# A hybrid decoder block: two orders pinned in the seven-product blocks, and a row factor with two sets of columns

## The chip, the cores and the metric

The kernel runs on one core of one Trainium2 chip. The metric is the device time of one execution in microseconds (us). The core's engines are TensorE (PE in the profile; PEld is its weight load), VectorE (DVE), ScalarE (ACT), GpSimd (POOL) and SyncE (SP), which here issues the loads of the weights.

## The reference

One layer over x of 256 tokens by 2048 channels, all in fp32: a half-step FFN, a mixer, a second half-step FFN, a final norm.

```python
def swiglu_ffn(x, w_gate, w_up, w_down):
    return (jax.nn.silu(x @ w_gate) * (x @ w_up)) @ w_down

x = x + 0.5 * swiglu_ffn(rms_norm(x, ffn1_norm), ffn1_w_gate, ffn1_w_up, ffn1_w_down)
z = rms_norm(x, mix_norm) @ w_in          # recurrent branch and short convolution follow
...
x = x + y @ w_out
x = x + 0.5 * swiglu_ffn(rms_norm(x, ffn2_norm), ffn2_w_gate, ffn2_w_up, ffn2_w_down)
return rms_norm(x, final_norm)
```

The gate and up weights are 2048 x 5632, the down weights 5632 x 2048.

## The kernel before

**The precision.** Every operand of a product is held as a high part (a cast to fp32r) and a low part (the rest). `parts_of` (line 170) makes both from a weight tile `raw` of 128 x 2048 elements, which is a block of 512 rows by 512 columns: ScalarE casts it in two halves (`hi`), then VectorE subtracts (`lo`). `multiply` (line 197) multiplies a weight block with 128 tokens in 12 matmuls: eight with the high part, for which the stationary operand is in turn the tokens' high and low part, then four with the low part. So TensorE meets the high part first and the low part 8 matmuls later.

**The seven products.** Gate and up weights are taken in 11 columns of 512 (`s` counts pairs of columns behind the first, 0 to 4), and in four row units of 512 (`u`). `seven` (line 345) does for a pair of columns and row units 0 and 1, with both halves of the tokens, what would be eight block products, by seven, with sums of weight blocks and prepared sums of the tokens (`sf`, tiles `xs`). Units 2 and 3 of the same columns go by `usual`, plain products for both token halves. The weight blocks are w11, w12 (unit 0, first and second column), w21, w22 (unit 1), and for the usual ones b2, a2 (unit 2), b3, a3 (unit 3). The program's order of one block is:

- p0: w11 into bank a (copied to d)
- w11 := w12 - w11 on VectorE, then p4 with it into bank c: the **second product**
- x01: b2 into banks e and c
- w11 := w22 - w11, then p5 into a
- x11: b3 into e and c
- w12 := w22 - w12, the **fourth's weight sum**, then p6 into a: the fourth product
- p2: w22 into c
- x00: a2 into d and a
- w11 := w21 - w11, then p3 into a; x10: a3 into a and d; p1: w21 into d

That is 180 matmuls. A block is named after its matrix, FFN and pair: g1_2 is the gate of FFN1, s = 2; u2_0 the up of FFN2, s = 0; d1_5 and the like are blocks of the down product. There are 20 of g and u and 6 of d. The tiles carry it: lo_g1_2_p4 is the low part of the second product of g1_2, raw_u1_1_01 the w12 of u1_1 (row unit, then column: 00 is w11, 01 w12, 11 w22, 10 w21, 21 and 31 are b2 and b3, 20 and 30 a2 and a3). In the profile the numbers of blocks are left out (lo_g_p, raw_u). Gate and up of a pair alternate: g1_0, u1_0, g1_1, u1_1 and on, with a block of the down product behind every second pair.

**Buffers and loads.** A load is 1 MB from the SP queue (line 165), in the order that the scheduler set; a load at the head of the queue waits until its buffer is free, and those behind it wait too. w11 and w12 lie in a pool of 2 (tag `kept`): the next block's w11 goes where this block's w12 lies and is free after lo p6; the next w12 goes where w11 lies and is free after lo p3. The others share a pool of 3 (tag `raw`). High and low parts have three buffers in turn.

**The order of work.** The program is written through wrappers whose call sits on line 43, so nearly all instructions of the profile carry L43, and tiles tell them apart. A scheduler sets the order of each engine by its own model of durations, with the dependences as bounds. `tc.keep_in_program_order(ins)` adds a bound: ins stays behind the instruction that the program wrote last before it for the same engine. Before the change this was used in `join` (line 440) and, for all instructions, at the start of FFN1 and at the end of the last down product.

**The row factor.** The mixer and FFN2 normalise after the product has begun. `Norm.rows` (line 254) spreads the factor of each token over the partitions: per token half it multiplies the identity by the factors (`diag`), and a matmul with ones puts the result on all 128 partitions (`pb`), which is copied to `bc`. The diagonal is one tile of 128 x 128 with a single buffer, so the second half's multiplication waits for the first half's matmul. It is called by `begin_after` (line 647, FFN2: tiles with n2) and in the mixer behind the first columns (line 1005: tiles with nm).

Of the kernel before, what the change touches and what calls it, by code (L numbers as in the profile page):

```python
# [10 lines left out]
F32 = mybir.dt.float32  # L11
# [3 lines left out]
ALU = mybir.AluOpType  # L15
AX = mybir.AxisListType

P = 128
# [31 lines left out]
def hybrid_block(ctx: ExitStack, tc: tile.TileContext, a: dict, out: bass.AP):  # L50
# [32 lines left out]
    def bank(name):  # L83
        return psum.tile([P, 512], F32, tag="ps", name=name)

    def f32(ap):
        return ap.bitcast(F32)
# [79 lines left out]
                loaded(i)  # L167
        return raw

    def parts_of(raw, name, pieces=((0, 2), (2, UK)), split=None):  # L170
        pool, bufs = splits, 2
        if extra:
            turn_of["split"] += 1
            if turn_of["split"] % 3 == 0:
                pool, bufs = extra[0], 1
        hi = pool.tile([P, UK, CW], F32R, tag="hi", name=f"hi_{name}", bufs=bufs)
        lo = pool.tile([P, UK, CW], F32R, tag="lo", name=f"lo_{name}", bufs=bufs)
        for i, e in pieces:
            if split:
                split(i)  # L180
            act.copy(hi[:, i:e, :], raw[:, i:e, :])
            if split:
                dve.tensor_tensor(lo[:, i:e, :], raw[:, i:e, :], f32(hi[:, i:e, :]), op=ALU.subtract)
        if not split:
            dve.tensor_tensor(lo, raw, f32(hi), op=ALU.subtract)
        return [(hi[:, j, :], lo[:, j, :]) for j in range(UK)]

    def unit(src, name):
# [26 lines left out]
    class Norm:  # L215
# [35 lines left out]
            dve.reduce_sum(tot, self.ss, axis=AX.X)  # L251
            self.r = inv_sqrt(tot, D, self.name)

        def rows(self):

            pb = bank(f"pb_{self.name}")
            for t in range(NT):
                dg = work.tile([P, P], F32, tag="diag", name=f"diag_{self.name}_{t}", bufs=1)
                dve.tensor_scalar(dg, ident, self.r[:, t : t + 1], None, op0=ALU.mult)
                pe.matmul(pb[:, t * P : (t + 1) * P], ones, dg, start=True, stop=True)  # L260
            self.bc = work.tile([P, S], F32, tag="bc", name=f"bc_{self.name}", bufs=1)
            dve.tensor_copy(self.bc, pb[:, :S])

# [81 lines left out]
    def seven(w, rows, cols, sf, xs, name, keep, done, between=None, ready=None, whole=True):  # L345
# [21 lines left out]
        def product_of(i, raw, ps, begin=False, end=True, blk=None):  # L367
            multiply([(ps, sf[i], begin, end)], blk or parts_of(raw, f"{name}_p{i}"), True)
# [8 lines left out]
        if whole:  # L377
            act.copy(d, a)
        dve.tensor_tensor(w11, w12, w11, op=ALU.subtract)
        product_of(4, w11, c, True)  # L380
        s5 = snap(c, "s5")
        if between:
            between(0)
# [7 lines left out]
            between(2)  # L391
        if two:
            usual(1, b3, 1, (e, 1, False, True), (c, 0, False, False))
        dve.tensor_tensor(w12, w22, w12, op=ALU.subtract)
        product_of(6, w12, a)
        u3 = snap(a, "u3")
        done(1, 1, e, [u3, s5])
# [11 lines left out]
    def ffn(tag, norm, after, opening=False):  # L409
        with (  # L410
# [232 lines left out]
            def begin_after():  # L643
                follow = {
                    (0, "g"): [flush],
                    (0, "u"): [norm.factor, lambda: plain(0)],
                    (1, "g"): [norm.rows, lambda: plain(1), lambda: normalise(0)],
                    (1, "u"): [lambda: normalise(1), sums, lambda: plain(2)],
                    (2, "g"): [lambda: normalise(2), lambda: plain(3)],
                }  # L650
# [168 lines left out]
    with tc.tile_pool(name="mixer", bufs=1) as mp, tc.tile_pool(name="mixw", bufs=2) as mw:  # L819
# [18 lines left out]
        def tmp(tag, name, w=S, dt=F32, bufs=2):  # L838
            return mw.tile([P, w], dt, tag=tag, name=f"{tag}_{name}", bufs=bufs)
# [160 lines left out]
        for i, (use, part, half) in enumerate(order):  # L1000
            ps = columns(w_in, part * (D // 2) + half * CW, nm.xT, f"in_{part}_{half}")
            if i == 0:
                flush()
                nm.factor()
                nm.rows()
                bc = nm.bc
                dve.tensor_tensor(bc2, bc, bc, op=ALU.mult)
                gate_weights("a", a["lru_w_a"][0])
                gate_weights("i", a["lru_w_i"][0])
                yT += [big(f"yT_{u}") for u in range(KD // UK)]  # L1010
            use(ps, half)
# [103 lines left out]
```

## Time and profile before

| | |
|---|---|
| time, median of 3 runs | 1723.59 us (1723.5 to 1724.75) |
| the profiled execution | 1723.6 us |
| its span | 1721.7 us |
| TensorE busy | 1703.6 us, 99% |
| VectorE busy | 1473.1 us, 86% |
| ScalarE busy | 1135.7 us, 66% |
| DMA, mean over the span | 206 GB/s |

The span runs from the first to the last instruction of the profiled execution; about 2 us lie around it. Rows of the timelines give the start, the time, the engine, the line, the operation, the written tile <- the tiles that were read, the shape, and the number of instructions in the row; square brackets hold the idle time ahead of them and what ended it. Matmuls of a row overlap: one of 512 columns begins some 0.227 us after the one before it, while each is listed with a longer duration. The list of waits has, for each kind, the sum, the times and the longest.

### The profile page before, as it was taken

The numbers are of one execution on the slowest core, as the hardware profiler recorded it, in microseconds if no ns is written. First come the engines' busy times: TensorE is split into PE (matmuls) and PEld (weight loads), VectorE is DVE, ScalarE is ACT, GpSimd is POOL, SyncE is SP. The second block draws the span as 40 slices with busy tenths as digits, with TensorE's granted clock in tenths as the row PEclk, the third lists the DMA queues.
The fourth block names the chain that finished last, engine by engine and source line by source line (L and its number), as shares of the span: only waits on it lengthen the run. The fifth ranks groups of instructions, "written<-read, shape, count | busy, mean of one in ns | idle before, by whom it ended". The sixth has DMA issues, their size and how long they took to land.

```text
span 1721.7 us, 20143 instructions
## 1 busy us (share of the span) xinstructions
PE 1703.6 (99%) x7859; PEld 1417.2 (82%) x7859; DVE 1473.1 (86%) x1210; ACT 1135.7 (66%) x1433; POOL 6.9 (0%) x32
## 2 busy tenths in 40 slices
PE   8999999999999999999999999999999999999998
PEld 6888888888888888888888888788888888888886
DVE  7998999989889878687987668989989888889796
ACT  6867667676568676575655456686567675667764
POOL 1000000000000000000000000000000000000000
PEclk9999999999999999999999999999999999999999
DMA  8666568585567684556555664685567666576863
GB/s 298 204 212 205 195 220 218 199 272 185 180 214 224 211 252 164 179 172 195 174 193 199 223 201 141 206 267 181 201 229 220 200 201 233 195 214 202 241 199 123
DMA packets 220383, 354.75 MB, mean 206 GB/s; under 512 B 52100, under 2 KB 54528, under 8 KB 220160
## 3 DMA queue, kind: packets, MB, share of 16 engines
q1 hardware_dynamic: 219824, 352.36, 63.4%
q8 instruction: 61, 1.00, 0.2%
q10 hardware_dynamic: 144, 1.05, 0.2%
q14 instruction: 34, 0.28, 0.0%
q0 software_dynamic: 320, 0.07, 0.0%
HBM read 339.82 MB, written 2.10 MB: 199 GB/s over the span
## 4 chain that ended last, share of the span: by engine, by line
PE 90%; DVE 4%; ACT 1%; issue 0%; DMA 0%; DVEq 0%; ACTq 0%
PE ps_d L43 14%; PE ps_in L43 13%; PE ps_u_a L43 8%; PE ps_g_a L43 8%; PE ps_u_c L43 6%; PE ps_g_c L43 6%; PE ps_d_a L43 5%; PE ps_o L43 5%; PE ps_g_d L43 4%; PE ps_u_d L43 3%; PE ps_d_c L43 3%; PE ps_u_e L43 3%; PE ps_g_e L43 3%; PE ps_d_d L43 3%; PE ps_d_e L43 2%; DVE lo_g_p L43 1%
## 5 line engine op out<-in xcount | busy, mean ns | idle before, releaser
L43 ACT CAST hi_u_p<-raw_u 128x1024 fp32r<-128x1024 f32 x140 | 141.8, 1048 | 52.7 <-DVE raw_u L43 14.7
L43 DVE TENSOR_TENSOR lo_u_p<-raw_u,hi_u_p 128x2048 fp32r<-128x2048 f32 x70 | 159.3, 2287 | 19.6 <-ACT hi_u_p L43 19.1
L43 ACT CAST hi_g_p<-raw_g 128x1024 fp32r<-128x1024 f32 x132 | 132.7, 1047 | 62.0 <-DVE raw_g L43 22.6
L43 DVE TENSOR_TENSOR lo_g_p<-raw_g,hi_g_p 128x2048 fp32r<-128x2048 f32 x66 | 150.2, 2287 | 21.3 <-ACT hi_g_p L43 21.3
L43 PE MATMUL ps_d<-hi_d,h 128*128 128x512 f32 x704 | 167.2, 389 | 0.0
L43 PEld LDWEIGHTS ps_d<-hi_d,h 128*128 128x128 f32 x704 | 132.1, 188 | 27.4
L43 PE MATMUL ps_in<-xT_nm,hi_in 128*128 128x512 f32 x640 | 153.9, 392 | 0.0
L43 PEld LDWEIGHTS ps_in<-xT_nm,hi_in 128*128 128x128 f32 x640 | 117.2, 188 | 23.0 <-ACT tha L43 0.4
L43 ACT CAST hi_d_p<-raw_d 128x1024 fp32r<-128x1024 f32 x84 | 85.8, 1048 | 72.6 <-DVE raw_d L43 29.8
L43 DVE TENSOR_TENSOR lo_d<-raw_d,hi_d 128x2048 fp32r<-128x2048 f32 x44 | 100.3, 2289 | 31.4 <-ACT hi_d L43 31.3
L43 ACT CAST hi_in<-raw_in 128x1024 fp32r<-128x1024 f32 x80 | 80.0, 1046 | 66.8 <-PE ps_in L43 45.4
L43 DVE TENSOR_TENSOR lo_in<-raw_in,hi_in 128x2048 fp32r<-128x2048 f32 x40 | 91.4, 2287 | 36.4 <-ACT hi_in L43 33.7
L43 ACT CAST hi_u_x<-raw_u 128x1024 fp32r<-128x1024 f32 x80 | 81.0, 1046 | 43.8 <-PE ps_u_c L43 23.1
L43 ACT CAST hi_d<-raw_d 128x1024 fp32r<-128x1024 f32 x88 | 88.8, 1045 | 22.1 <-PE ps_d_d L43 10.0
L43 DVE TENSOR_TENSOR raw_u<-raw_u,raw_u 128x2048 f32<-128x2048 f32 x40 | 91.6, 2291 | 13.5 <-DMA raw_u<-in_ffn_w_up_dram 12.9
L43 DVE TENSOR_TENSOR lo_d_p<-raw_d,hi_d_p 128x2048 fp32r<-128x2048 f32 x42 | 96.1, 2288 | 7.7 <-ACT hi_d_p L43 7.6
L43 ACT CAST hi_g_x<-raw_g 128x1024 fp32r<-128x1024 f32 x80 | 81.2, 1046 | 23.9 <-PE ps_g_c L43 12.8
L43 DVE TENSOR_TENSOR lo_g_x<-raw_g,hi_g_x 128x2048 fp32r<-128x2048 f32 x40 | 91.5, 2287 | 4.8 <-ACT hi_g_x L43 4.5
L43 DVE TENSOR_TENSOR lo_u_x<-raw_u,hi_u_x 128x2048 fp32r<-128x2048 f32 x40 | 91.5, 2287 | 1.7 <-ACT hi_u_x L43 1.6
L43 DVE TENSOR_TENSOR raw_g<-raw_g,raw_g 128x2048 f32<-128x2048 f32 x37 | 84.6, 2287 | 3.4 <-DMA raw_g<-in_ffn_w_gate_dram 3.1
L43 PE MATMUL ps_d<-lo_d,h 128*128 128x512 f32 x352 | 87.3, 389 | 0.0
L43 PEld LDWEIGHTS ps_in<-xT_nm,lo_in 128*128 128x128 f32 x640 | 82.2, 191 | 3.2
(392 smaller groups left out, 3644.7 us busy)
## 6 DMA issues: line engine op xcount, KB each, us to landing
raw_d<-in_ffn_w_down_dram SPq DMA_DIRECT2D x88, 1024.0 KB, 5.7
raw_u<-in_ffn_w_up_dram SPq DMA_DIRECT2D x87, 1024.0 KB, 5.3
raw_g<-in_ffn_w_gate_dram SPq DMA_DIRECT2D x86, 1024.0 KB, 5.4
raw_in<-in_w_in_dram SPq DMA_DIRECT2D x40, 1024.0 KB, 5.1
raw_o<-in_w_out_dram SPq DMA_DIRECT2D x16, 1024.0 KB, 5.1
xres<-in_x_dram SPq DMA_DIRECT2D x4, 512.0 KB, 7.6
raw_u<-in_ffn_w_up_dram SPq DMA_DIRECT2D x2, 512.0 KB, 9.4
raw_g_first<-in_ffn_w_gate_dram SPq DMA_DIRECT2D x1, 1024.0 KB, 12.1
```

Of the source, the lines that this page charges most:

```text
L43: ins = getattr(self.engine, name)(*args, **kwargs)
```

## The change

Three edits. `parts_of` gets an argument that pins the subtraction of the low part in program order; `seven` calls it so for the second product. The fourth's weight sum is pinned as well, at its place in the program, behind what the program wrote last for VectorE before it: the low part of x11, or of p5 where there is no x11. And `Norm.rows` takes one tile of 128 x 512 for both diagonals, from a pool of the caller (`keep` in FFN2, the tag `half` in the mixer), with columns of their own for each token half.

```diff
-    def parts_of(raw, name, pieces=((0, 2), (2, UK)), split=None):
+    def parts_of(raw, name, pieces=((0, 2), (2, UK)), split=None, held=False):
...
-            dve.tensor_tensor(lo, raw, f32(hi), op=ALU.subtract)
+            ins = dve.tensor_tensor(lo, raw, f32(hi), op=ALU.subtract)
+            if held:
+                tc.keep_in_program_order(ins)
...
-        def rows(self):
-
-            pb = bank(f"pb_{self.name}")
+        def rows(self, room):
+
+            pb, dg = bank(f"pb_{self.name}"), room(f"diag_{self.name}")
             for t in range(NT):
-                dg = work.tile([P, P], F32, tag="diag", name=f"diag_{self.name}_{t}", bufs=1)
-                dve.tensor_scalar(dg, ident, self.r[:, t : t + 1], None, op0=ALU.mult)
-                pe.matmul(pb[:, t * P : (t + 1) * P], ones, dg, start=True, stop=True)
+                o = slice(t * P, (t + 1) * P)
+                dve.tensor_scalar(dg[:, o], ident, self.r[:, t : t + 1], None, op0=ALU.mult)
+                pe.matmul(pb[:, o], ones, dg[:, o], start=True, stop=True)
...
         dve.tensor_tensor(w11, w12, w11, op=ALU.subtract)
-        product_of(4, w11, c, True)
+        product_of(4, w11, c, True, blk=parts_of(w11, f"{name}_p4", held=True))
...
-        dve.tensor_tensor(w12, w22, w12, op=ALU.subtract)
+        tc.keep_in_program_order(dve.tensor_tensor(w12, w22, w12, op=ALU.subtract))
         product_of(6, w12, a)
...
-                    (1, "g"): [norm.rows, lambda: plain(1), lambda: normalise(0)],
+                    (1, "g"): [lambda: norm.rows(keep), lambda: plain(1), lambda: normalise(0)],
...
-                nm.rows()
+                nm.rows(lambda name: tmp("half", name, bufs=4))
```

Before the change the scheduler put the fourth's sum right behind the first difference, ahead of the low part of p4, in nearly all blocks. With the pins much else stands elsewhere too. Three places follow.

TensorE in g1_2, from the second product to the low part of p5, before the change (bank a, c or e; xs1_0 is a sum of tokens, x1_2 and x1_3 are units 2 and 3):

```order
L43 MATMUL ps_g1_2_c_2145<-hi_g1_2_p4_2183,xs1_0_434 128x512 x8
L43 MATMUL ps_g1_2_e_2146<-hi_g1_2_x01_2202,x1_2_202 128x512
L43 MATMUL ps_g1_2_c_2145<-lo_g1_2_p4_2184,xs1_0_434 128x512 x4
L43 MATMUL ps_g1_2_e_2146<-hi_g1_2_x01_2202,x1_2_202 128x512 x7
L43 MATMUL ps_g1_2_e_2146<-lo_g1_2_x01_2203,x1_2_202 128x512
L43 MATMUL ps_g1_2_c_2145<-hi_g1_2_x01_2202,x1_2_202 128x512 x8
L43 MATMUL ps_g1_2_e_2146<-lo_g1_2_x01_2203,x1_2_202 128x512 x3
L43 MATMUL ps_g1_2_c_2145<-lo_g1_2_x01_2203,x1_2_202 128x512 x4
L43 MATMUL ps_g1_2_a_2144<-hi_g1_2_p5_2238,xs1_0_434 128x512 x8
L43 MATMUL ps_g1_2_e_2146<-hi_g1_2_x11_2257,x1_3_203 128x512 x7
L43 MATMUL ps_g1_2_a_2144<-lo_g1_2_p5_2239,xs1_0_434 128x512 x4
```

The same stretch of TensorE in the changed kernel:

```order
L43 MATMUL ps_g1_2_c_2145<-hi_g1_2_p4_2183,xs1_0_434 128x512 x8
L43 MATMUL ps_g1_2_c_2145<-lo_g1_2_p4_2184,xs1_0_434 128x512 x4
L43 MATMUL ps_g1_2_e_2146<-hi_g1_2_x01_2202,x1_2_202 128x512 x8
L43 MATMUL ps_g1_2_c_2145<-hi_g1_2_x01_2202,x1_2_202 128x512 x8
L43 MATMUL ps_g1_2_e_2146<-lo_g1_2_x01_2203,x1_2_202 128x512 x4
L43 MATMUL ps_g1_2_c_2145<-lo_g1_2_x01_2203,x1_2_202 128x512 x4
L43 MATMUL ps_g1_2_a_2144<-hi_g1_2_p5_2238,xs1_0_434 128x512 x8
L43 MATMUL ps_g1_2_a_2144<-lo_g1_2_p5_2239,xs1_0_434 128x512 x4
L43 MATMUL ps_g1_2_e_2146<-hi_g1_2_x11_2257,x1_3_203 128x512 x8
```

The single matmul of x01 between the high and the low part of p4 is gone, and so are the seven matmuls of x11 between the high and the low part of p5.

VectorE in u1_2, from the first difference (tile 00 from 01 and 00) on, before the change; raw_u1_2_01 as the written tile is the fourth's sum:

```order
L43 TENSOR_TENSOR raw_u1_2_00_2439<-raw_u1_2_01_2441,raw_u1_2_00_2439 128x2048
L43 TENSOR_TENSOR raw_u1_2_01_2441<-raw_u1_2_11_2445,raw_u1_2_01_2441 128x2048
L43 TENSOR_TENSOR lo_u1_2_p4_2475<-raw_u1_2_00_2439,hi_u1_2_p4_2474 128x2048
L43 TENSOR_TENSOR lo_u1_2_x01_2494<-raw_u1_2_21_2443,hi_u1_2_x01_2493 128x2048
L43 TENSOR_TENSOR raw_u1_2_00_2439<-raw_u1_2_11_2445,raw_u1_2_00_2439 128x2048
L43 TENSOR_TENSOR lo_u1_2_p5_2524<-raw_u1_2_00_2439,hi_u1_2_p5_2523 128x2048
L43 TENSOR_TENSOR lo_u1_2_x11_2543<-raw_u1_2_31_2447,hi_u1_2_x11_2542 128x2048
L43 TENSOR_TENSOR lo_u1_2_p6_2573<-raw_u1_2_01_2441,hi_u1_2_p6_2572 128x2048
L43 TENSOR_TENSOR lo_u1_2_p2_2595<-raw_u1_2_11_2445,hi_u1_2_p2_2594 128x2048
L43 TENSOR_TENSOR raw_u1_2_00_2439<-raw_u1_2_10_2451,raw_u1_2_00_2439 128x2048
```

The same ten instructions of VectorE in the changed kernel:

```order
L43 TENSOR_TENSOR raw_u1_2_00_2439<-raw_u1_2_01_2441,raw_u1_2_00_2439 128x2048
L43 TENSOR_TENSOR lo_u1_2_p4_2475<-raw_u1_2_00_2439,hi_u1_2_p4_2474 128x2048
L43 TENSOR_TENSOR raw_u1_2_00_2439<-raw_u1_2_11_2445,raw_u1_2_00_2439 128x2048
L43 TENSOR_TENSOR lo_u1_2_x01_2494<-raw_u1_2_21_2443,hi_u1_2_x01_2493 128x2048
L43 TENSOR_TENSOR lo_u1_2_p5_2524<-raw_u1_2_00_2439,hi_u1_2_p5_2523 128x2048
L43 TENSOR_TENSOR lo_u1_2_x11_2543<-raw_u1_2_31_2447,hi_u1_2_x11_2542 128x2048
L43 TENSOR_TENSOR raw_u1_2_01_2441<-raw_u1_2_11_2445,raw_u1_2_01_2441 128x2048
L43 TENSOR_TENSOR raw_u1_2_00_2439<-raw_u1_2_10_2451,raw_u1_2_00_2439 128x2048
L43 TENSOR_TENSOR lo_u1_2_p6_2573<-raw_u1_2_01_2441,hi_u1_2_p6_2572 128x2048
L43 TENSOR_TENSOR lo_u1_2_p2_2595<-raw_u1_2_11_2445,hi_u1_2_p2_2594 128x2048
```

The fourth's sum went from the second place to the seventh, the second difference (tile 00 from 11) ahead of the low part of x01, and the last difference (from tile 10, the w21) ahead of the low part of p6.

VectorE at the end of g1_1, before the change, from the low part of p6 to the first low part of the next block:

```order
L43 TENSOR_TENSOR lo_g1_1_p6_1724<-raw_g1_1_01_1592,hi_g1_1_p6_1723 128x2048
L43 TENSOR_TENSOR lo_g1_1_p2_1746<-raw_g1_1_11_1596,hi_g1_1_p2_1745 128x2048
L43 TENSOR_TENSOR lo_g1_1_x00_1765<-raw_g1_1_20_1600,hi_g1_1_x00_1764 128x2048
L43 TENSOR_TENSOR raw_g1_1_00_1590<-raw_g1_1_10_1602,raw_g1_1_00_1590 128x2048
L43 TENSOR_TENSOR u3_g1_1_1740<-u3_g1_1_1740,s5_g1_1_1642 128x512
L43 TENSOR_TENSOR u3_g1_1_1740<-ps_g1_1_e_1588,u3_g1_1_1740 128x512
L43 TENSOR_TENSOR u2_g1_1_1691<-ps_g1_1_c_1587,u2_g1_1_1691 128x512
L43 TENSOR_TENSOR lo_g1_1_p3_1795<-raw_g1_1_00_1590,hi_g1_1_p3_1794 128x2048
L43 TENSOR_TENSOR lo_g1_1_x10_1812<-raw_g1_1_30_1604,hi_g1_1_x10_1811 128x2048
L43 TENSOR_TENSOR lo_g1_1_p1_1843<-raw_g1_1_10_1602,hi_g1_1_p1_1842 128x2048
L43 TENSOR_TENSOR lo_u1_1_p0_1882<-raw_u1_1_00_1865,hi_u1_1_p0_1881 128x2048
```

The same stretch in the changed kernel, from the fourth's sum on:

```order
L43 TENSOR_TENSOR raw_g1_1_01_1592<-raw_g1_1_11_1596,raw_g1_1_01_1592 128x2048
L43 TENSOR_TENSOR lo_g1_1_p2_1746<-raw_g1_1_11_1596,hi_g1_1_p2_1745 128x2048
L43 TENSOR_TENSOR lo_g1_1_p6_1724<-raw_g1_1_01_1592,hi_g1_1_p6_1723 128x2048
L43 TENSOR_TENSOR lo_g1_1_x00_1765<-raw_g1_1_20_1600,hi_g1_1_x00_1764 128x2048
L43 TENSOR_TENSOR u3_g1_1_1740<-u3_g1_1_1740,s5_g1_1_1642 128x512
L43 TENSOR_TENSOR raw_g1_1_00_1590<-raw_g1_1_10_1602,raw_g1_1_00_1590 128x2048
L43 TENSOR_TENSOR u3_g1_1_1740<-ps_g1_1_e_1588,u3_g1_1_1740 128x512
L43 TENSOR_TENSOR u2_g1_1_1691<-ps_g1_1_c_1587,u2_g1_1_1691 128x512
L43 TENSOR_TENSOR lo_g1_1_x10_1812<-raw_g1_1_30_1604,hi_g1_1_x10_1811 128x2048
L43 TENSOR_TENSOR lo_g1_1_p3_1795<-raw_g1_1_00_1590,hi_g1_1_p3_1794 128x2048
L43 TENSOR_TENSOR lo_g1_1_p1_1843<-raw_g1_1_10_1602,hi_g1_1_p1_1842 128x2048
L43 TENSOR_TENSOR lo_u1_1_p0_1882<-raw_u1_1_00_1865,hi_u1_1_p0_1881 128x2048
```

The sum stands here now, ahead of the low part of p2, and the low part of p3 has gone behind that of x10. So have the low parts of p3 in g1_0 and g2_1; in g2_0 they stood so before. On SP's queue the loads behind g1_1 came in the order w11 of u1_1, a3 of g1_1, b2, w12, w22 of u1_1; now they come as a3 of g1_1, then w11, b2, w22, w12 of u1_1.

## The prediction

> **What bounds the kernel now.** I read the page first: the busy line of the engines and the clock line.
>
> ```profile
> PE 1703.6 (99%) x7859; PEld 1417.2 (82%) x7859; DVE 1473.1 (86%) x1210; ACT 1135.7 (66%) x1433; POOL 6.9 (0%) x32
> ...
> PEclk9999999999999999999999999999999999999999
> ```
>
> TensorE works for 99% of the span at a full clock. So the end can only move by what is added to or taken from its waits, since the diff leaves its 7859 matmuls as they are. The table by windows, over the stretches of FFN1 and FFN2 in which the seven-product blocks run, says how close VectorE is behind (columns: span, PE, PEld, DVE, ACT, POOL busy, clock, DMA share, GB/s):
>
> ```profile
> 80.00:700.00 620.00, 619.27 (x2731) 510.72 (x2731) 544.39 (x357) 420.49 (x487) 0.00 (x0) 1.00 0.66 212
> 1070.00:1710.00 640.00, 637.87 (x2806) 525.37 (x2806) 565.10 (x361) 434.50 (x504) 0.00 (x0) 1.00 0.65 206
> ```
>
> TensorE idles 0.7 and 2.1 us there; VectorE is busy 88% of the time, so it has 12% of slack, some 5 us in a block of about 41 us (180 matmuls at 0.227 us, the pitch in the rows below). The list of TensorE's waits holds all that an edit could win:
>
> ```profile
> PE ps_g_c L43 <- DVE lo_g_p L43: 1.5, 4, 0.4
> PE ps_u_c L43 <- ACT hi_u_p L43: 0.8, 1, 0.8
> ...
> PE ps_u_c L43 <- DVE lo_u_p L43: 0.6, 1, 0.6
> PE pb_nm L43 <- DVE diag_nm L43: 0.4, 1, 0.4
> ```
>
> The first row is the low part of the second product, late in four gate blocks (g1_2, g1_4, g2_2, g2_4); the next two are one block, u2_0; the last is the row factor. Together 3.3 us, 0.2% of the time. There is little to win, and every block is a chance to lose.
>
> **The second product's low part.** VectorE's timeline of g1_2, then TensorE's:
>
> ```profile
> 282.29 4.61 DVE L43 TENSOR_TENSOR raw_g<-raw_g,raw_g 128x2048 f32<-128x2048 f32 x2
> ...
> 287.41 2.28 DVE L43 TENSOR_TENSOR lo_g_p<-raw_g,hi_g_p 128x2048 fp32r<-128x2048 f32 x1
> ```
>
> ```profile
> 287.18 1.98 PE L43 MATMUL ps_g_c<-hi_g_p,xs 128*128 128x512 f32 x8
> 288.99 0.39 PE L43 MATMUL ps_g_e<-hi_g_x,x 128*128 128x512 f32 x1
> 289.75 1.20 PE L43 MATMUL ps_g_c<-lo_g_p,xs 128*128 128x512 f32 x4 [0.37 <-DVE lo_g_p L43]
> ...
> 296.14 2.13 PE L43 MATMUL ps_g_a<-hi_g_p,xs 128*128 128x512 f32 x8
> 298.11 1.75 PE L43 MATMUL ps_g_e<-hi_g_x,x 128*128 128x512 f32 x7
> 299.70 1.07 PE L43 MATMUL ps_g_a<-lo_g_p,xs 128*128 128x512 f32 x4
> ```
>
> The x2 in the first row is the first difference and, right behind it, the fourth's sum. The low part then ends at 289.69 and TensorE, with one filler matmul, waits for it. With the sum taken out from between, the low part can end one VectorE step (2.2 us from start to start) earlier, at 287.5, while the eight high matmuls end at 289.0: the wait goes. From start to start the sequence loses 0.53 at the low part (289.75 against 288.99 + 0.227) and about 0.26 in the eight high matmuls and the filler behind (296.14 to 298.11 is 1.97 where 8 x 0.227 is 1.82; the same again ahead of it): 0.8 us per block. In g1_4 and g2_4 that is won whole: **-1.6**. In g1_2 and g2_2 the order of TensorE loses its seven filler matmuls between the high and low parts of p5 (7 x 0.227 = 1.6 us of cover). The low part of p5 is two casts and a subtraction behind its difference; without the filler TensorE would stand before it some 0.7 to 1.1 us. I count these two blocks as **0**; bounds -0.8 and +1.1 each.
>
> **The row factor.** With two columns' ranges the second multiplication no longer waits for the first matmul; the 0.4 us wait in pb_nm goes: **-0.4**. pb_n2 has no row among the waits: 0. If the new room had to wait for a buffer, it would be for one eviction of 0.68 us, so at worst +0.3.
>
> **The sum in its new place.** It now stands behind the low parts of p5 and x11, just ahead of p6, which needs it. VectorE's rows of g1_1 and of u1_2, then TensorE's need of the low part of p6 in u1_2:
>
> ```profile
> 215.50 2.29 DVE L43 TENSOR_TENSOR lo_g_x<-raw_g,hi_g_x 128x2048 fp32r<-128x2048 f32 x1
> 217.70 4.49 DVE L43 TENSOR_TENSOR lo_g_p<-raw_g,hi_g_p 128x2048 fp32r<-128x2048 f32 x2
> ```
>
> ```profile
> 337.32 2.29 DVE L43 TENSOR_TENSOR lo_u_x<-raw_u,hi_u_x 128x2048 fp32r<-128x2048 f32 x1
> ...
> 345.06 2.29 DVE L43 TENSOR_TENSOR raw_u<-raw_u,raw_u 128x2048 f32<-128x2048 f32 x1 [1.05 <-DMA raw_u<-in_ffn_w_up_dram]
> ```
>
> ```profile
> 347.07 1.07 PE L43 MATMUL ps_u_a<-lo_u_p,xs 128*128 128x512 f32 x4
> ```
>
> In g1_1, behind the low part of x11 (217.7) come sum, low p2, low p6: 219.9, 222.1, 224.3. TensorE wants low p6 at about 223.9: late by 0.45. In u1_2 the order puts the last difference ahead of low p6, and that difference waits for w21. If low x11 still ends at 337.3 at the earliest, the load goes then, lands 5.4 us later (as it did in before, from the end of low x11, 339.6, to 345.0), the difference ends at 345.2 and low p6 at 347.5: late by 0.45. g2_1, u2_2 and u2_3 have the same orders: 5 x 0.45 = **+2.2**; bounds 0 (casts already lie ahead, VectorE idled 2.1 us in this stretch and may use it) and 0.9 each.
>
> **The load that comes later.** The low part of p3 ends the life of a buffer that the next block's w12 is loaded into. In g1_0, g1_1 and g2_1 the new order puts low p3 behind low x10, and on SP's queue w12 goes behind w22. VectorE's and TensorE's rows at that place, and ScalarE's casts:
>
> ```profile
> 228.93 2.29 DVE L43 TENSOR_TENSOR lo_g_p<-raw_g,hi_g_p 128x2048 fp32r<-128x2048 f32 x1 [0.20 <-ACT hi_g_p L43]
> 231.92 2.29 DVE L43 TENSOR_TENSOR lo_g_x<-raw_g,hi_g_x 128x2048 fp32r<-128x2048 f32 x1 [0.69 <-ACT hi_g_x L43]
> ```
>
> ```profile
> 246.38 1.98 PE L43 MATMUL ps_u_c<-hi_u_p,xs 128*128 128x512 f32 x8
> 248.19 1.07 PE L43 MATMUL ps_u_c<-lo_u_p,xs 128*128 128x512 f32 x4
> ```
>
> ```profile
> 241.53 2.00 ACT L43 CAST hi_u_p<-raw_u 128x1024 fp32r<-128x1024 f32 x2 [0.70 <-DVE raw_u L43]
> ...
> 244.39 0.59 ACT L43 ACTIVATE z<-ps_g_d 128x512 f32<-128x512 f32 x1
> ```
>
> What such a late load does is in the trace already, in u2_0, whose predecessor has this order in before. The chain's DMA row, VectorE and TensorE there, and the page's median for such a load:
>
> ```profile
> 1102.30 7.15 DMA raw_u<-in_ffn_w_up_dram
> ```
>
> ```profile
> 1109.54 2.29 DVE L43 TENSOR_TENSOR raw_u<-raw_u,raw_u 128x2048 f32<-128x2048 f32 x1 [2.87 <-DMA raw_u<-in_ffn_w_up_dram]
> ```
>
> ```profile
> 1110.40 1.98 PE L43 MATMUL ps_u_a<-hi_u_p,x 128*128 128x512 f32 x8
> ...
> 1114.08 2.15 PE L43 MATMUL ps_u_c<-hi_u_p,xs 128*128 128x512 f32 x8 [0.80 <-ACT hi_u_p L43]
> ...
> 1119.09 1.19 PE L43 MATMUL ps_u_c<-lo_u_p,xs 128*128 128x512 f32 x4 [0.59 <-DVE lo_u_p L43]
> ```
>
> ```profile
> raw_u<-in_ffn_w_up_dram SPq DMA_DIRECT2D x87, 1024.0 KB, 5.3
> ```
>
> Two loads side by side take 7.15 us instead of 5.3. The first difference begins only 0.86 us ahead of the block's first matmul, and TensorE waits 0.80 + 0.59. For u1_1 after the change: low p3 (the first VectorE row, 228.93) takes the place of low x10 (231.92) and would end at 234.2; the sum has come into this stretch as well, of whose 2.2 us I take 0.7 as not absorbed by the gaps: 234.9. The load of 7.15 lands at 242.1, the difference (2.29) ends at 244.4, the two casts (2.0) with an activation (0.6) among them at 247.0, low p4 (2.29) at 249.3. TensorE wants the low part at 248.2, or at 248.6 with the highs' own delay: about 0.7 late there. The differences behind it, each with two casts and a low part, come later by the same amount and find less cover: another 0.6 in p5, and 1.2 in p6, ahead of which the sum now stands too. That is 2.5 by the long sum and 1.4 by the u2_0 row; I take 2.0 for each of u1_0, u1_1 and u2_1: **+6.0**; bounds 0.5 and 2.8 each.
>
> Here a rule of the Trainium skill speaks, "DMA: Bandwidth & Descriptors", section "Issuing engines are not separate DMA queues": transfers end up on the same 16 engines and interleave. The trace agrees (7.15 against 5.3 us). If they did not, the load would land at 240.2 and these three losses would shrink to about 0.5 in all, the whole sum to 1724; by the rule and by the row it stays as above.
>
> **Sum**: -1.6 + 0 - 0.4 + 2.2 + 6.0 = +6.2 on the profiled execution's 1723.6 us, which is also the median of the runs (1723.59): **1729.8**. Not counted: g2_0 (its p5 has fewer fillers, up to +0.65), d2_9 (about 0.5), u2_0's own 1.4 us, which stay. With the bounds of the forecast's terms, 1726 to 1735.
>
> **Rivals.**
> A. The change does what it says, and the slack of VectorE (12%) takes up the rest: the load of w12 lands by 240 although low p3 went back, because low x10 does not wait in front of it. Then all four waits go (-3.2), and pb_nm's 0.4; if u2_0 mends too, -1.4: 1718.6, else 1720. For it: VectorE has gaps of 2.1 to 2.9 us in the very rows above. Against it: three blocks have u2_0's order. It decides at a landing of 241 in u1_1.
> B. The waits only change places: -3.2 - 0.4 against 3 x 0.7 for late loads and 5 x 0.3 for low p6: 1723.6, say 1724. The bound is TensorE's stream, and every other term small.
> C. VectorE falls behind in many blocks: the late loads at their upper 2.8 (8.4), low p6 and similar products late by 0.9 in nine blocks (8.1), gains of 2.0: 1738. Against it: 12% of slack, and no block now carries its delay to the next one.
> D. A wait of a late load reaches 3 us and TensorE's clock falls. That price is in the start of this kernel:
>
> ```profile
> 5.83 1.97 PE L43 MATMUL pt_n<-ident,xres 128*128 128x128 f32 x8 [3.11 <-DMA xres<-in_x_dram]
> ...
> 9.04 1.05 PE L43 MATMUL ps_g<-hi_g_start,xT_n 128*128 128x512 f32 x2
> 9.89 0.63 PE L43 MATMUL ps_g<-lo_g_start,xT_n 128*128 128x512 f32 x1
> ```
>
> Behind an idle time of 3.11 us, two matmuls took 0.85 us from 9.04 to 9.89, 0.42 each instead of 0.227; that lasts to about 11, some 5 us, of which 2.4 are lost. Three blocks with 3.1 + 2.4 instead of 2.0 give 1740. The largest wait in a block is 0.80, so it is unlikely. The Trainium skill, "TensorE: Matmul & The Clock Gate", section "HAM oscillation — how this bites in real kernels", puts the point at idle gaps over about 3.4 us; the row above shows a slow start behind 3.11, though it is also the start of the program.
>
> **How the numbers follow.** Forecast .57, A .13, B .18, C .10, D .02. What a measurement of this kernel can tell from no change is 0.2%, 3.4 us: 1720.1 to 1727.0. Faster: the better half of A, .08. Same: the rest of A (.05), B (.18), and the forecast's lower end (.07): .30. Slower: .50 + .10 + .02 = .62. The range runs from 1721 to 1737: it leaves out most of A, half of C, and D, together under .2.
>
> **What would show it.** In the profile after, the row of ps_g_c waiting for lo_g_p should shrink from four waits to none or two, pb_nm's should be gone, and rows of ps_u_c waiting for hi_u_p and lo_u_p should stand at u1_0, u1_1 and u2_1 with 1 to 3 us each, behind a first difference that waited for the DMA. ps_a waits for low p6 of 0.3 to 0.9 should stand in the g1_1 and u1_2 kinds of block. If there are no waits for w12, A is right; if the waits are there, but at 0.7 in all per block, B. I am wrong outright if TensorE's busy time or clock differs, for its work is the same.

## The result and the profile after

The changed kernel takes **1750.3 us** (median of 4 runs, 1747.2 to 1754.63) against 1723.57 us before: ratio 1.0157, 95% interval 1.0145 to 1.0169, 26.7 us slower. That lies outside the range on record. The profiled execution is the slowest of the four, 1754.6 us with a span of 1752.5 us, 30.8 us longer than before's.

The page's busy line and one row of its groups, and TensorE's list of waits in the changed kernel:

```profile
PE 1717.4 (98%) x7859; PEld 1418.7 (81%) x7859; DVE 1468.8 (84%) x1210; ACT 1132.9 (65%) x1433; POOL 7.0 (0%) x32
...
L43 DVE TENSOR_TENSOR lo_u_p<-raw_u,hi_u_p 128x2048 fp32r<-128x2048 f32 x70 | 159.4, 2288 | 37.8 <-ACT hi_u_p L43 37.7
```

```profile
PE ps_d_d L43 <- ACT hi_d_x L43: 2.8, 2, 1.4
PE ps_u_a L43 <- DVE lo_u_p L43: 2.6, 5, 0.9
...
PE ps_u_c L43 <- ACT s_u L43: 2.5, 2, 1.9
PE ps_g_c L43 <- ACT s_g L43: 2.3, 3, 0.8
PE ps_u_c L43 <- DVE lo_u_p L43: 2.0, 4, 0.9
PE ps_d_a L43 <- DVE hs L43: 1.8, 2, 1.2
...
PE ps_g_c L43 <- DVE lo_g_p L43: 1.1, 1, 1.1
```

VectorE's waits ahead of the low parts lo_u_p, before, then after:

```profile
DVE lo_u_p L43 <- ACT hi_u_p L43: 19.1, 14, 2.1
```

```profile
DVE lo_u_p L43 <- ACT hi_u_p L43: 37.7, 24, 3.1
```

The engines do the same work. VectorE is even less busy, and stands idle ahead of the low parts lo_u_p for 37.7 us instead of 19.1. TensorE has many small waits of several kinds, and its busy time has grown by 13.8 us though its matmuls are the same. To see where the time lies, I sum for each block the time from the start of one matmul to the next beyond the median for its shape, a figure worked out from all TensorE rows of the trace. The columns behind the first two are runs of the experiments below. Each column is one execution, up to 4.4 us away from the median of its kernel:

| blocks | before | after | gu_pins | s5_first | swap | busy_behind | back_diff_copy |
|---|---|---|---|---|---|---|---|
| d1_1 + d2_1 | 0.1 | 10.9 | 2.3 | 3.4 | 2.2 | 2.4 | 0.8 |
| u1_2 + u2_2 | -0.1 | 5.4 | 4.4 | -0.1 | 1.3 | 1.5 | 1.3 |
| g1_2 + g2_2 | 1.8 | 4.1 | 3.6 | 4.2 | 5.0 | 5.7 | 3.1 |
| g1_4 + g2_4 | 1.8 | 3.9 | 3.7 | 3.5 | 4.3 | 5.7 | 5.5 |
| u1_1 + u2_1 | -0.1 | 3.8 | -0.1 | -0.1 | 1.3 | 1.7 | 1.2 |
| u1_4 + u2_4 | -0.1 | 1.9 | 2.2 | 0.0 | 1.3 | 1.5 | 1.6 |
| u1_0 | -0.1 | 1.3 | 1.6 | 1.3 | 1.2 | 1.4 | 3.8 |
| g1_1 + g2_1 | 0.0 | 0.7 | 0.6 | 3.8 | 3.3 | 5.8 | 3.3 |
| all else | 7.9 | 10.1 | 6.5 | 8.1 | 20.1 | 19.2 | 8.7 |
| sum | 11.3 | 42.0 | 24.8 | 24.0 | 39.9 | 44.8 | 29.3 |

The difference of the sums, 30.7, is the difference of the spans but for rounding. Two blocks hold a third of it. Three kinds of place can be read directly.

**An empty gap.** VectorE in u2_2, before and after, from the first difference on:

```profile
1334.87 4.62 DVE L43 TENSOR_TENSOR raw_u<-raw_u,raw_u 128x2048 f32<-128x2048 f32 x2
1339.41 2.28 DVE L43 TENSOR_TENSOR lo_u_p<-raw_u,hi_u_p 128x2048 fp32r<-128x2048 f32 x1
```

```profile
1361.13 2.29 DVE L43 TENSOR_TENSOR raw_u<-raw_u,raw_u 128x2048 f32<-128x2048 f32 x1
1365.53 2.29 DVE L43 TENSOR_TENSOR lo_u_p<-raw_u,hi_u_p 128x2048 fp32r<-128x2048 f32 x1 [2.12 <-ACT hi_u_p L43]
```

The low part of p4 needs ScalarE's two casts of the difference. Before, the sum (the second of the x2) ran while ScalarE cast, and the low part followed 4.54 us behind the start of the difference. After, VectorE waits 2.12 us, and the low part follows after 4.40 us. It has gained 0.14 us, and the sum now needs 2.2 us of its own further on. Counted from all VectorE rows, the changed kernel idles 1.9 us or more ahead of low p4 in 18 of the 26 blocks; before, it did in none.

**ScalarE's queue.** ScalarE in u2_2 after, then TensorE (s_u is the copy s5 of bank c, in front of which x01 must not write there):

```profile
1367.78 0.59 ACT L43 COPY ps_u_d<-ps_u_a 128x512 f32<-128x512 f32 x1
1370.24 1.99 ACT L43 CAST hi_u_p<-raw_u 128x1024 fp32r<-128x1024 f32 x2 [1.87 <-DVE raw_u L43]
1372.14 0.58 ACT L43 COPY s_u<-ps_u_c 128x512 f32<-128x512 f32 x1
```

```profile
1368.91 1.99 PE L43 MATMUL ps_u_e<-hi_u_x,x 128*128 128x512 f32 x8
1372.77 3.68 PE L43 MATMUL ps_u_c<-hi_u_x,x 128*128 128x512 f32 x8 [1.87 <-ACT s_u L43]
1376.29 1.10 PE L43 MATMUL ps_u_e<-lo_u_x,x 128*128 128x512 f32 x4
```

Bank c was complete at 1368.9. The copy stands behind the casts for p5, and these wait for VectorE's second difference. So TensorE waits 1.87 us for a copy of 0.58. Its next eight matmuls then take 3.52 us to the following row instead of 1.82.

**The down blocks d1_1 and d2_1.** VectorE in d1_1, the hidden sum before (hs are the sums of hidden tokens that are the stationary operands of p5, p6 and p2), then VectorE, ScalarE and TensorE after:

```profile
174.79 0.68 DVE L43 TENSOR_TENSOR hs<-s_g,hs 128x512 fp32r<-128x512 f32 x1
```

```profile
178.71 2.28 DVE L43 TENSOR_TENSOR raw_d<-raw_d,raw_d 128x2048 f32<-128x2048 f32 x1
180.91 0.68 DVE L43 TENSOR_TENSOR hs<-s_g,hs 128x512 fp32r<-128x512 f32 x1
```

```profile
176.72 0.62 ACT L43 CAST hs<-z 128x512 fp32r<-128x512 f32 x1
181.09 2.95 ACT L43 CAST hi_d_p<-raw_d 128x1024 fp32r<-128x1024 f32 x3 [3.75 <-DVE raw_d L43]
```

```profile
181.65 1.88 PE L43 MATMUL ps_d_a<-hi_d_p,hs 128*128 128x512 f32 x7 [1.15 <-DVE hs L43]
...
186.50 0.73 PE L43 MATMUL ps_d_d<-hi_d_x,h 128*128 128x512 f32 x2 [1.39 <-ACT hi_d_x L43]
...
187.88 3.14 PE L43 MATMUL ps_d_a<-hi_d_p,hs 128*128 128x512 f32 x8
```

Before, the hidden sum that p5 needs ran at 174.79. Now the fourth's sum (178.71) stands in front of it, TensorE waits 1.15 us, and ScalarE waits 3.75 us for it with the casts for p6, with p2's and x00's behind them.

### The profile page after: what moved, and what is told of

Its sections match the earlier page's. It is cut to its first block, busy times and chain, and to the rows that moved or that the text cites. A ratio compares the mean times of both kernels' runs of the same rounds, so it can differ in the third digit from the quotient of the medians.

```text
span 1752.5 us, 20119 instructions
## 1 busy us (share of the span) xinstructions
PE 1717.4 (98%) x7859; PEld 1418.7 (81%) x7859; DVE 1468.8 (84%) x1210; ACT 1132.9 (65%) x1433; POOL 7.0 (0%) x32
## 5 line engine op out<-in xcount | busy, mean ns | idle before, releaser
L43 DVE TENSOR_TENSOR lo_u_p<-raw_u,hi_u_p 128x2048 fp32r<-128x2048 f32 x70 | 159.4, 2288 | 37.8 <-ACT hi_u_p L43 37.7
L43 DVE TENSOR_TENSOR lo_g_p<-raw_g,hi_g_p 128x2048 fp32r<-128x2048 f32 x66 | 149.9, 2286 | 19.3 <-ACT hi_g_p L43 19.1
```

The source lines that it names most:

```text
L43: ins = getattr(self.engine, name)(*args, **kwargs)
```

## The experiments

All of VectorE's and ScalarE's orders below are read from the built programs. One of them stands in for a run: with the pin on the low part of p4 alone, no instruction of the four engines changes its place. So the pin on the sum is what moved the orders in the blocks. No run was made of either pin alone.

### The row factor alone

The edit is `Norm.rows` and its two calls as in the change, nothing else. 

> The kernel before with the row factor's two sets of columns alone. My theory (nearly all of the loss comes from the place of the fourth's sum): the 0.4 us wait of pb_nm goes and nothing else moves, 1723.2 us, ratio 0.9998, inside what can be told from no change. Rival (the new room for the diagonals, or its order in the mixer, costs a part of the loss): 1726 or more.

1723.22 us, ratio 0.9999 (0.9990 to 1.0008). The wait of pb_nm is gone from the list; the 0.4 us is too little to be seen in the time. The loss is not here.

### Where the pins are, and one queue

gu_pins leaves both pins off in the six down blocks:

```diff
-        product_of(4, w11, c, True, blk=parts_of(w11, f"{name}_p4", held=True))
+        product_of(4, w11, c, True, blk=parts_of(w11, f"{name}_p4", held=name[0] != "d"))
...
-        tc.keep_in_program_order(dve.tensor_tensor(w12, w22, w12, op=ALU.subtract))
+        total = dve.tensor_tensor(w12, w22, w12, op=ALU.subtract)
+        if name[0] != "d":
+            tc.keep_in_program_order(total)
```

> The changed kernel with both pins left off in the six blocks of the down product. In the changed kernel's trace the blocks d1_1 and d2_1 hold 6.0 and 4.9 us that they did not hold before. If these come from the sum pinned there, in front of the sums of the hidden tokens and of the casts behind it: 10.8 us less, about 1739.5. Rival (they come from VectorE being late as a whole, carried over from the blocks ahead): both blocks still wait, 1748 or more.

1737.32 us, 1.0084 (1.0070 to 1.0097), 13.0 us less than the changed kernel. d1_1 and d2_1 give back 8.6 us; u1_1 and u2_1, with one block between, give back all of their 3.9.

s5_first queues the casts of p5 behind the copy s5 (`taken` keeps that instruction):

```diff
-        product_of(5, w11, a)
+        with tc.issue_after(taken["s5"].ins):
+            blk = parts_of(w11, f"{name}_p5")
+        product_of(5, w11, a, blk=blk)
```

> The changed kernel with the casts of the third weight sum (p5) queued behind the copy of bank c (s5) on ScalarE. My theory: the five waits for this copy (g1_2, u1_2, g2_2, u2_2, g2_3; 7.5 us with the slow matmuls behind the one of 1.87 us) come from ScalarE's order alone and go; in d1_1 and d2_1 the order now also lets the hidden sums go ahead, which takes some of their 10.8 us: 1733 to 1743. Rival (VectorE is late anyway, the copy only shows it first): the same time is waited for the low parts of p5 and p6, 1748 or more.

1735.48 us, 1.0067 (1.0052 to 1.0082), 14.8 less. The waits for the copy in u1_2, u2_2 and g2_3 are gone. Those in g1_2 and g2_2 stay (these two blocks lose 4.2 us), and g1_4 and g2_4 now have such a wait too, of 0.85 and 0.82 us: in these four the copy waits behind other casts and copies. Since the scheduler planned the rest anew, d1_1 and d2_1 gave back 7.5 as well.

gu_s5 is both together. 

> Both repairs together: the pins left off in the blocks of the down product, and the casts of p5 queued behind the copy of bank c on ScalarE. If the two losses are apart: the waits for that copy in the run without the pins there (some 7 us) go from its 1737.3: about 1730. Rival (they share their time, one repair takes what the other took): 1735 or more.

1734.61 us, 1.0061 (1.0045 to 1.0077). That is the rival's number but for 0.4 us: the two do not add up. With each edit the scheduler moves other things, and what is mended in one block appears in another (g1_2 and g2_2: 7.2 us in the profiled execution, which is 4.9 us above the median).

### The sum bound behind the low part of p4 only

```diff
-                tc.keep_in_program_order(ins)
+                low["p4"] = ins
...
-        tc.keep_in_program_order(dve.tensor_tensor(w12, w22, w12, op=ALU.subtract))
+        with tc.issue_after(low["p4"].ins):
+            dve.tensor_tensor(w12, w22, w12, op=ALU.subtract)
```

`low["p4"]` is the subtraction that makes the low part; its own pin is left off here. 

> The changed kernel, but with the fourth's sum bound only behind the low part of p4, not behind what the program wrote last for VectorE; the scheduler puts it right behind that low part in the blocks with x11. My theory (the late place costs, not that the low part of p4 goes first): the waits for low p4 in the four gate blocks go and the new ones don't come, 1719 to 1724. Rival (taking the sum from between the first difference and the low part costs, wherever it goes): 1735 or more.

1742.18 us, 1.0107 (1.0093 to 1.0121): my theory of the late place fell, and the kernel still loses 18.6 us. By the built orders the sum stands right behind low p4 in 13 of the 26 blocks and 3 to 12 places behind it in the others, and the scheduler planned the rest anew, so the run does not say how much of this is the sum's.

### One move, all else held

To keep the scheduler out, the following kernels give each of the four engines a written order, by edges from each instruction to the next (`in_order`; `ORDERS` holds the place of every instruction): that of the kernel before, with a stated move.

```diff
     with the program of before, at the end of hybrid_block:
+    in_order(tc, ORDERS)
...
swap, on VectorE in 24 blocks:  w11 := w12 - w11 | w12 := w22 - w12 | low p4
                            ->  w11 := w12 - w11 | low p4 | w12 := w22 - w12
late, on VectorE in 25 blocks:  w12 := w22 - w12 behind the later of low p5 and low x11
```

> The kernel before with the order of TensorE, VectorE, ScalarE and SyncE written down as the scheduler had made it, and one thing moved: in 24 of the 26 blocks the fourth's sum changes places with the low part of p4. Nothing else moves. My theory now (the idea itself is sound, and the loss comes from all that the scheduler moved with it, ScalarE's queue above all): the four waits for low p4 go, 0.8 us each, and no new wait comes: 1720.4. Rival (a sum one step later is late for p6 or pushes the differences behind it, as it seems where it was bound behind low p4 alone): new waits of 0.3 to 1 us in most blocks, 1730 or more.

1753.03 us, 1.0176 (1.0162 to 1.0191). The theory of "all that moved with it" fell too, and the rival held: the exchange alone loses 29.6 us. 

> The kernel before with all four orders written down, and only the fourth's sum moved in 25 blocks to where the changed kernel has it, behind the later of the low parts of p5 and x11. My theory (the late place by itself is cheap where ScalarE's queue does not hold the copy of bank c behind the casts for p6; only d1_1 and d2_1 have these casts ahead of the copy, and wait some 4 us each; the four waits for low p4 go): 1727 to 1733. Rival (the late place itself makes the loss, through low p6 in every block): 1745 or more.

1774.75 us, 1.0300 (1.0284 to 1.0315): the sum at the place that the changed kernel gives it, with all else as before, loses 51.3 us. Of the 55.7 us in the trace, 21.2 lie in d1_1 and d2_1, by the mechanism that was expected there, but twice as large. Another 22.0 lie in g1_2, g1_4, g2_2 and g2_4, where TensorE waits up to 2.6 us for ScalarE's casts for p4. So the time is the rival's, but not through low p6. ScalarE and TensorE in d1_1 of late:

```profile
183.61 1.04 ACT L43 CAST hi_d_p<-raw_d 128x1024 fp32r<-128x1024 f32 x1 [5.30 <-DVE raw_d L43]
184.56 0.58 ACT L43 COPY s_d<-ps_d_c 128x512 f32<-128x512 f32 x1
```

```profile
185.19 3.78 PE L43 MATMUL ps_d_c<-hi_d_x,h 128*128 128x512 f32 x8 [7.78 <-ACT s_d L43]
```

A cast that waits 5.3 us for the late sum holds a copy of 0.58 us, and TensorE waits 7.78 for it.

### Is it the gap?

The swap showed what I had not weighed: the gap. VectorE's waits for ScalarE's casts ahead of lo_u_p, in swap, then in swap_gap, which puts a useless step of 2.29 us where the sum had been:

```profile
DVE lo_u_p L43 <- ACT hi_u_p L43: 37.9, 22, 2.1
```

```profile
DVE lo_u_p L43 <- ACT hi_u_p L43: 18.7, 13, 2.1
```

```diff
         dve.tensor_tensor(w11, w12, w11, op=ALU.subtract)
+        if name not in ("g2_0", "u2_0"):
+            dve.reduce_sum(idle, w11, axis=AX.XY)
swap_gap:    w11 := w12 - w11 | reduce_sum | low p4 | w12 := w22 - w12
busy_behind: w11 := w12 - w11 | w12 := w22 - w12 | low p4 | reduce_sum
```

These two do more than the reference asks: the reduction's result is used nowhere. 

> The run called swap, with an additional useless reduction of the first difference (128x2048 elements, its result is used nowhere) on VectorE between the first difference and the low part of p4 in the same 24 blocks, where the sum stood before. My theory now (the sum used the time in which VectorE has to wait for ScalarE's two casts of the difference anyway; without it VectorE stands idle there for 2.1 us): the reduction is free, 1750 to 1756 as swap. Rival (the low part of p4 does come earlier when nothing stands between): the reduction pushes it back, 1765 or more.

1759.96 us, 1.0210 (1.0196 to 1.0224): between the two expectations, 6.9 us over swap, 0.3 us for each of the 24 steps of 2.29 us. The gap is nearly, not quite, free: in the u blocks VectorE's idle time falls back to what it was, while in g1_2, g1_4, g2_2 and g2_4, where a step on z shares the gap, the low part is pushed back by 0.7 us. 

> The kernel before with its four orders written down, the sum where it was, and the same useless reduction of about 2.2 us on VectorE right behind the low part of p4 in 24 blocks. My theory (swap's loss is that of 2.2 us of VectorE's time put behind low p4, while the gap in front of it stays empty): the same loss as swap, 1745 to 1760. Rival (swap loses because the sum itself is late for p6): here the sum is on time and VectorE's 12% of slack takes the reduction, 1723 to 1730.

1761.77 us, 1.0228 (1.0212 to 1.0244), just above what was expected. Here the sum has its old place and is never late, and a step that means nothing costs 38.2 us behind low p4. Most of its blocks lose the same as in swap_gap, one by one (u1_2 + u2_2 1.5 in both, d1_1 + d2_1 2.4 and 2.3). So a late sum is not needed for the loss: 2.2 us of VectorE's time behind low p4 are enough.

The same useless step in the six blocks where the second difference and low p5 stand side by side, once in the gap between them, once behind low p5: 

> The kernel before with its four orders written down, and a useless reduction of 2.2 us on VectorE between the second difference and the low part of p5 in the six blocks where these two stand side by side (g1_1, u1_2, u1_4, g2_1, u2_2, u2_4) and VectorE waits 2.12 us for ScalarE's casts. My theory (VectorE's time in such a gap is free): no change, 1722.5 to 1725. Rival (an instruction of 2.2 us costs wherever it stands, by the slack of VectorE as a whole): as busy_behind per block, 1.6 us each, 1731 or more.

1723.19 us, 1.0001 (0.9991 to 1.0011). VectorE in u1_2 of busy_gap:

```profile
330.77 2.28 DVE L43 TENSOR_TENSOR raw_u<-raw_u,raw_u 128x2048 f32<-128x2048 f32 x1
333.09 2.29 DVE L43 TENSOR_REDUCE idle<-raw_u 128x1 f32<-128x2048 f32 x1
335.30 2.28 DVE L43 TENSOR_TENSOR lo_u_p<-raw_u,hi_u_p 128x2048 fp32r<-128x2048 f32 x1
```

The low part starts at 335.30, as against 335.11 before. The gap swallows 2.2 us. 

> The same reduction in the same six blocks, but one step later, behind the low part of p5. My theory (outside a gap VectorE's time is not free): 1 to 2 us per block, 1729 to 1736. Rival (VectorE's 12% of slack take it): 1722.5 to 1725.

1725.48 us, 1.0012 (1.0002 to 1.0021): 0.35 us per block, nearly the rival's number, and my theory of 1 to 2 us per block fell. In the trace the six blocks lose at most 0.2 us each, though the low part of x11 behind the step comes 2.2 us later; the one new wait, 0.70 us, is in d1_5. So there is slack at this place outside the gap too, and this pair of runs does not show that a gap is cheaper than another place. What counts is the slack at the place, not VectorE's share of idle time.

How much slack there is can be read at the next meeting with TensorE. In u2_2 of before, low p5 and the matmuls that use it:

```profile
1348.28 2.29 DVE L43 TENSOR_TENSOR lo_u_p<-raw_u,hi_u_p 128x2048 fp32r<-128x2048 f32 x1 [2.12 <-ACT hi_u_p L43]
```

```profile
1352.08 1.07 PE L43 MATMUL ps_u_a<-lo_u_p,xs 128*128 128x512 f32 x4
```

It is ready at 1350.57 and wanted at 1352.08: 1.51 us of slack for a step of 2.2, so 0.69 late. The swap lost 0.70 in that block (0.64 against -0.06).

### Half a sum

In g1_2, g1_4, g2_2, g2_4 alone, half the sum stays in the gap and half goes behind low p4, with before's orders held:

```diff
-        dve.tensor_tensor(w12, w22, w12, op=ALU.subtract)
+        if name in ("g1_2", "g1_4", "g2_2", "g2_4"):
+            for i in (0, 2):
+                dve.tensor_tensor(w12[:, i : i + 2], w22[:, i : i + 2], w12[:, i : i + 2], op=ALU.subtract)
+        else:
+            dve.tensor_tensor(w12, w22, w12, op=ALU.subtract)
```

> The kernel before with its four orders written down; in the four gate blocks that waited for low p4 (g1_2, g1_4, g2_2, g2_4) the sum is made in two halves of 1.1 us, one where it was, the other behind low p4. My theory (the gap that ScalarE's casts leave is wide enough for half a sum and the z step, and the rest of the block has 0.4 us to give): the four waits go, 0.8 us each, 1720.4. Rival (the low part of x01 behind it has no slack): the same time is waited there, 1723 to 1726.

1723.65 us, 1.0001 (0.9992 to 1.0010): the rival. The four waits for low p4 are gone and four for low x01, next on VectorE, have taken their place. It also shows that writing the orders down costs nothing that the time can show. TensorE's list in halves:

```profile
PE ps_g_e L43 <- DVE lo_g_x L43: 2.1, 4, 0.5
```

### The changed kernel's orders, with single moves undone

These start from the changed kernel's own orders, written down.

```diff
after_back:      w12 := w22 - w12 back between the first difference and low p4 (24 blocks)
after_copy:      ScalarE: copy s5 ahead of the casts for p5 (u1_2, u2_2, u2_3, u2_4)
after_diff:      w11 := w21 - w11 back behind low p6 and low p2 (20 blocks)
back_diff:       after_back and after_diff
back_diff_copy:  all three
```

> The changed kernel with the order of its four engines written down as its scheduler made it, and only the fourth's sum put back on VectorE between the first difference and the low part of p4 in 24 blocks. My theory (the changed kernel's loss is the gap in front of low p4 that stays empty, 2.1 us of VectorE in most blocks, and what that makes late): most of the 26.7 us go, 1723 to 1731. Rival (the loss is in the orders that the scheduler chose anew for ScalarE and SyncE, which stay here): 1738 or more.

1760.67 us, 1.0213 (1.0199 to 1.0227): 10.4 us worse than the changed kernel, so filling the gap does not heal it. VectorE's list shows one reason:

```profile
DVE raw_u L43 <- DMA raw_u<-in_ffn_w_up_dram: 42.4, 14, 6.3
```

In 18 blocks the scheduler has put the last difference, which needs w21's load, ahead of low p6. Without the sum in front, VectorE comes to it sooner and stands there for the load. 

> The changed kernel with its four orders written down, and on ScalarE alone the copy of bank c (s5) put ahead of the casts for p5 in u1_2, u2_2, u2_3 and u2_4. The sum stays late. If ScalarE's order holds the time by itself: the waits of 0.8 us in u1_2 and 1.9 us in u2_2 go with the 2 us of slow matmuls behind the second, 1745 to 1746. Rival (VectorE is late and the copy only shows it): the low parts of p5 and p6 are waited for instead, 1749 or more.

1751.30 us, 1.0162 (1.0148 to 1.0175): no gain. The rival was right for this one: TensorE waits for the low part of p6 instead, 1.77, 2.07 and 1.39 us in u1_2, u2_2 and u2_3. 

> The changed kernel with its orders written down, and on VectorE alone the last difference (w21 - w11) put back behind the low parts of p6 and p2 in the 20 blocks where it had come ahead of one of them. The sum stays late. Theory A (the last difference, which waits for the load of w21, holds low p6 back): the waits for low p6 go, some 5 us, 1743 to 1747. Theory B (the late sum alone makes low p6 late): no change, 1749 to 1753.

1749.20 us, 1.0147 (1.0130 to 1.0164): 1.1 us less, inside the intervals of both, theory B's number; not a cause by itself. 

> The run called after_back with the last difference put back too: the sum in the gap, the last difference behind low p6 and p2, all else as the changed kernel has it. Theory A (VectorE's order makes the loss by these two moves together, and after_back kept its loss because with the sum gone the last difference stood before low p6 all the longer, waiting for w21): 1726 to 1734. Theory B (the loss is in ScalarE's, TensorE's and SyncE's orders): 1742 or more.

1745.96 us, 1.0133 (1.0118 to 1.0149): 14.7 less than after_back, 4.3 less than the changed kernel; theory B's number. 

> As back_diff, and on ScalarE the copy of bank c ahead of the casts for p5 in u1_2, u2_2, u2_3 and u2_4. Theory A with ScalarE's order as the third part: 2 to 5 us less than back_diff, 1723 to 1730. If that order does not count once VectorE is in time: the same as back_diff.

1742.08 us, 1.0108 (1.0093 to 1.0123): 3.9 less again, so the copies do count once these two moves on VectorE are undone. 8.2 of the 26.7 us are undone by these three moves; 18.5 remain, in small waits in most blocks.

## Why the prediction was wrong

**The step that failed** is the price of the sum's move. The prediction took it as a loss in five blocks where low p6 would be late by 0.45, and as 0.7 us "not absorbed by the gaps" in the three with a late load. In the other 18 blocks, the six of the down product among them, it put the price at nothing; the ground that it gives is VectorE's 12% of slack. With all else held, swap and busy_behind put the price of VectorE's time behind low p4 at 30 to 38 us, and late, with the sum at the place that the changed kernel gives it, at 51.3.

The reading that led there is this: "With the sum taken out from between, the low part can end one VectorE step (2.2 us from start to start) earlier, at 287.5". It asked what VectorE had to do, not what the low part had to wait for. ScalarE's row in g1_2 of before stood in the trace:

```profile
284.71 1.99 ACT L43 CAST hi_g_p<-raw_g 128x1024 fp32r<-128x1024 f32 x2
```

The casts end at 286.70 and the low part began at 287.41: at most 0.7 us could be won, not 2.2. In swap, counted from the first difference, the low part came 0.7 to 0.8 us sooner in g1_2, g1_4, g2_2 and g2_4, 1.3 in g1_1 and g2_1, and 0.1 or nothing in 17 of the other 18 blocks, where VectorE then idled 2.1 us or more. So in most blocks the sum had filled a gap in which VectorE had to stand anyway, and taking it out won next to nothing.

Point by point:

- **Low p4, -1.6 in g1_4 and g2_4.** Wrong: g1_4 went from 0.9 to 2.7, g2_4 from 0.9 to 1.2. In g1_2 and g2_2, counted as 0, the wait for low p4 went, but waits for the copy s5 and low p5 came, and they lost 0.9 and 1.4. In halves the waits for low p4 go as well, and the same time is then waited for low x01.
- **The row factor, -0.4.** The wait went, as stated; the size is below what a time can show.
- **Low p6 in five blocks, +2.2.** Right in four: low p6 is 0.2 to 0.5 us late in g1_1, u1_2, g2_1 and u2_3, 1.7 us in all with a slower matmul behind each. In u2_2 it is in time.
- **Late w12, +6.0.** u1_0, u1_1 and u2_1 lost 5.3, and their first differences waited 1.6, 1.5 and 2.3 us for the load. But in gu_pins, with waits of 1.4 and 1.8 for the same load, u1_1 and u2_1 lost nothing. The size came out, and waits for low p4, p5 and p6 stand where they were expected (in u1_1 and u2_1 the longest is for low p6, 0.85 and 0.87); but that the load is the cause in these two is not shown.
- **Left out.** The down blocks d1_1 and d2_1 (10.8 us, 8.6 of them undone by gu_pins) and ScalarE's order, in which the copy s5 fell behind the casts for p5 in u1_2, u2_2 and u2_3, and between them in u2_4. I compared the orders of TensorE, VectorE and SyncE and took ScalarE's for granted. Rival C had the right direction and half the size.
- **Rival D, .02.** In no block did a wait of TensorE reach 3 us, but matmuls did slow down, behind shorter waits than it put in (below).
- **The sign of being wrong outright** came: TensorE's busy time rose by 13.8 us. The work is the same 7859 matmuls. Some 4.5 us are slow matmuls; most of the rest is the part of each wait that the busy line cannot show, since a matmul of 512 columns is listed as 0.39 us while the next could begin after 0.227.
- **The range.** The bounds of the terms, added up, give 1721.5 to 1737.4, not 1726 to 1735; the result lies outside both.

What is shown: the pin on the sum makes the loss; the row factor alone loses nothing in its run, and the pin on low p4 alone moves no instruction. VectorE's step behind low p4 costs 30 us and more by itself. Filling the gap again inside the changed kernel's orders does not heal it. What stays open: how the remaining 18.5 us divide among the other orders. No run separates these: with one engine's order from the changed kernel and the others' from the kernel before, instructions would wait for each other in a circle.

## What to carry to other kernels

Before moving an instruction out of the way of another, look at what the other waits for: an instruction that stands in the shadow of another engine's work is nearly free there, and elsewhere costs what the slack does not cover. Here that was 1.2 us of 2.2 per block behind low p4 (swap), and 0.35 behind low p5 (busy_past). The busy share (88% here) does not say what a step costs; the slack at the next meeting with the bound engine does (1.5 us against 2.2 in u2_2). And where a scheduler sets the order, compare every engine's queue: a copy of 0.6 us behind a cast that waits cost more than any of the waits that the change was aimed at.

## What the runs showed of the hardware

TensorE's matmuls slowed from 0.227 to about 0.43 us each behind some waits much shorter than the 3.1 us at the start. In the changed kernel a wait of 1.87 us was followed by eight such matmuls (u2_2: 1.7 us lost), in swap one of 2.15. In d1_1 waits of 1.15, 0.16, 1.39 and 0.32 us within 7 us were followed by them, in u1_0 of back_diff_copy waits of 0.48 and 1.14 within 2.8 us. In d1_1, d2_1 and u2_2 together this is some 4.5 of the changed kernel's 30.8 us.

The length of a wait does not settle it. Single waits of 1.53 to 1.62 us (gu_pins, sum_free, swap) had no slow matmuls behind them, and neither had waits of 2.08 and 2.23 us in g1_2 and g1_4 of late, nor those of 1.15, 0.16 and 1.39 us in d1_1 of after_diff. What else decides is not shown. It may be part of why the changed kernel's four runs spread over 7 us where before's agree within 1.3: the slowest has a granted clock of 0.996, the others 0.998. Only the slowest one's trace is kept.
